# Layer ends rebuilt in a Hawk / latent-attention / PEER trunk on one core: quarter tiles, squares on GpSimd, later weight splits, rotation inside the scores' contraction

## The chip, the core and the metric

The kernel runs on one core of a Trainium2 chip. A core has TensorE (PE, with its weight loads shown apart as PEld), VectorE (DVE), ScalarE (ACT), GpSimd (POOL), SyncE (SP, which here only starts transfers) and 16 DMA engines. The metric is the time of one execution on the device in microseconds; it was run three times before the change, and once more under the profiler.

## The reference

512 tokens of 1024 channels pass through one recurrent layer (RG-LRU), a PEER layer, one latent-attention layer (MLA) and a second PEER layer. Each sub-layer normalises its input, scales and shifts it by a conditioning vector ("ada"), and adds its result, times a gate, to the stream x. Cut to what the change touches:

```python
for l in range(2):
    mod = silu(c) @ ada_w[l] + ada_b[l]           # 6 x 1024: sh1 sc1 g1 sh2 sc2 g2
    h = rmsnorm(x, norm_mix_g[l]) * (1 + sc1) + sh1
    y = rglru_block(h) if l == 0 else mla_block(h)
    x = x + g1 * y
    h = rmsnorm(x, norm_ffn_g[l]) * (1 + sc2) + sh2
    x = x + g2 * peer(h)
return rmsnorm(x, final_g)

# mla_block, 16 heads of 64 + 32 query channels over a shared latent
q = (rmsnorm(h @ w_dq) @ w_uq)                    # q_nope 64, q_rope 32
s = (q_nope @ k_nope.T + rope(q_rope) @ rope(k_rope).T) * SCALE
# peer, 8 heads: 16 best of 128 x 128 experts by product keys
out = sum_k  g_k * gelu(h . u[idx_k]) * v[idx_k]
```

## The kernel before, in words

All values are kept transposed: channels on the 128 partitions, 512 tokens along the row, so x is eight tiles of 128x512. Matrix products are done in float32 by three passes (`mm3`, lines L187 to L189): each operand is split into a high part, rounded by ACT (L162, `whi`, `vh`, `hh`), and a low part, the difference, made by DVE or POOL (L163, `wlo`, `vl`, `hl`); PE multiplies high by low, low by high, high by high into one bank. `wtile` loads a weight tile and splits it; `split` is the split alone.

The work is written as five stages in a row, rglru, peer0, mla, peer1 and final. A scheduler with a model of each engine's times sets each engine's order from the dependences, the buffer counts and a few anchors (`tc.issue_after(instruction)` keeps what stands in it behind that instruction, on the same engine).

A norm needs the sum of squares over all 1024 channels. `residual` (L282) adds a bank's result into one tile of x, `sum_sq` squares the tile on ACT (L224, L225: `nacc`, `sq`) and adds it to `nacc` on DVE (L226); when all eight are in, `col_sums` sums over the partitions on PE (L232, `st`), ACT takes the square root (L243, `rcol`), DVE the reciprocal (L244), and PE spreads it to all partitions (L247, `rs`). Then DVE normalises (L257, `xn`), and ACT and DVE make `hh` and `hl`, the operands of the next product. This chain stands at the end of each stage, and the next stage's matmuls need it.

At the end of **rglru** (about 100 to 206 us of the span) PE makes per head the two gates' inputs (`ri`) and, between heads, an output gate (`gate`), then the output product (`wo`). DVE meanwhile runs the recurrence, and after the last split of y ten rows of the ada product: each loads 512 KB (`ada_raw`) and reduces 128x1024 against c (`ada_junk`, L151), with two buffers. Two weight tiles of the next stage (`wpq0`, 128x1024) are split by ACT and DVE there.

**peer** scores the keys (`pq`), takes the best 16, builds gates, computes expert activations in a dense form (`u`) and sums values: 128 value tiles `vraw` are loaded by SP, split, and multiplied by the split activations `al`, `ah` into six banks `acc` (three blocks of 128 tokens by two halves of 512 channels; the fourth block, `gacc`, is gathered by POOL and summed on DVE). Of the last two tiles ("held") the first half is multiplied at once and the second half after it; then `emit` copies the banks to `onat` (ACT and DVE), `finish(c)` transposes one of eight column blocks on PE (`ot`), adds it into x and squares it. Other work is spread over peer0's value loop: ada rows, and `positions` (`ps_...`), which makes the rotation's table and the mask and writes them to scratch in memory.

**mla** multiplies the normalised x to latents, rotates the shared 32 key channels, then for each of 16 heads makes q (`q`), rotates it, splits it to `qt`, and multiplies with `kt` (the scores, `s`, a contraction of 96 rows: 64 plain, 32 rotated). The 32 rotated channels come twice out of the product, plain in rows 64 to 95 and with halves swapped in rows 96 to 127; the rotation is rows 64 to 95 times a cosine table, plus rows 96 to 127 times a sine table: ACT copies `q` to `qf` (L644), then three operations of 32x512 follow (L646 to L648), on DVE for the first two heads and on POOL for the others. POOL also makes the low parts of mla's weights.

Of the kernel before, what the change touches and what calls it, by code (L numbers as in the profile page):

```python
# [9 lines left out]
F32 = mybir.dt.float32  # L10
# [39 lines left out]
HT = 8  # L50
RAWS = 4
GROWS = 4
LAST = 2
WF = 2
GSCALE = 16384.0

# [25 lines left out]
class Trunk:  # L82
# [137 lines left out]
    def sum_sq(self, sq, ch, k):  # L220
# [4 lines left out]
        last = nc.scalar.activation(sq, ch, AF.Square).ins  # L225
        nc.vector.tensor_tensor(self.nacc, self.nacc, sq, op=OP.add)  # L226
        return last

    def col_sums(self):
        self.sums = self.bank("st")  # L230
# [104 lines left out]
    def rglru(self):  # L335
        nc, io, tc = self.nc, self.io, self.tc
        with tc.tile_pool(name="lru", bufs=52) as pool, ExitStack() as st:
# [87 lines left out]
            ys = []  # L425
            for hd in range(4):
                gates(hd)
                gate(3 + hd)
                for j in (2 * hd, 2 * hd + 1):
                    last = decay(j)  # L430
                if hd == 3:
                    gate(KC - 1)
                if hd % 2 == 0:
                    continue
                js = range(2 * hd - 2, 2 * hd + 2)
                for j in js:
                    with tc.issue_after(last):
                        last2 = nc.scalar.activation(tt[j], tt[j], AF.Sqrt, scale=-1.0, bias=self.tiny).ins
                for j in js:
                    nc.vector.tensor_tensor(tt[j], tt[j], rr[j], op=OP.mult)  # L440
                    nc.vector.tensor_tensor(tt[j], tt[j], ig[j], op=OP.mult)
                    nc.vector.tensor_tensor_scan(tt[j], aa[j], tt[j], initial=0.0, op0=OP.mult, op1=OP.add)
                    with tc.issue_after(last2):
                        last_gelu = nc.scalar.activation(gg[j], gg[j], AF.Gelu).ins
                    nc.vector.tensor_tensor(tt[j], tt[j], gg[j], op=OP.mult)
                    ys.append(self.pair(pool, "y"))
                    lo = self.split(ys[j][0], ys[j][1], tt[j]).ins
            with tc.issue_after(conv):
                self.adas(6, late)
            with tc.issue_after(lo):  # L450
                self.adas(10, late)
            outs = [self.bank("wo") for _ in range(KC)]
            ws = []
            for k in range(KC):
# [90 lines left out]
    def mla(self):  # L545
        nc, io, tc = self.nc, self.io, self.tc
        with tc.tile_pool(name="mla", bufs=12) as pool, ExitStack() as st:
# [4 lines left out]
            mb = one([P, NB, T], BF, "mask_b")  # L552
            ckv = [(one([P, T], F32R, f"ckvh{m}"), one([P, T], F32R, f"ckvl{m}")) for m in range(2)]
            qlat = [(one([P, T], F32R, f"qlh{m}"), one([P, T], F32R, f"qll{m}")) for m in range(3)]
            nc.scalar.dma_start(rt, self.rscr)
            nc.scalar.dma_start(mb, self.mscr)
            gk = self.gain("gs_kv", self.vecr("kv_norm_g", 0, KC), self.mod[:, 104:112])
            gs = self.gain("gs_m1", self.vecr("norm_mix_g", KC, KC), self.mod[:, 56:64])
# [1 line left out]
            with tc.tile_pool(name="mlah", bufs=34) as hp:  # L560
                xn, hk = [], []
                for k in range(KC):
                    xn.append(self.normed(hp, k, rs))
                    hk.append(self.affine(hp, k, xn[k], gk, self.mod[:, 96:104])[1])
                    if k == KC - 2:
                        after = self.last
                outs = [self.bank("lat"), self.bank("lat"), self.bank("kr")]
                self.lin_k(outs[:2], [self.wtile(io["w_dkv"][m], KC, eng=nc.vector) for m in range(2)], hk)
                self.lin(outs[2], self.wtile(io["w_kr"], KC, eng=nc.vector), hk)
                wdq = [self.wtile(io["w_dq"][m], KC, pool=hp) for m in range(2)]  # L570
                krf = pool.tile([P, T], F32, name="krf", tag="t")
                nc.scalar.activation(krf, outs[2], AF.Copy)
                with tc.issue_after(after):
                    hq = [self.affine(hp, k, xn[k], gs, self.mod[:, 48:56], None if k < 6 else self.pair(pool, "hm"), 0, True)[1]
                          for k in range(KC)]
                kr2 = pool.tile([P, T], F32, name="kr2", tag="t")
                nc.gpsimd.tensor_tensor(kr2[64:96], krf[96:128], rt[96:128], op=OP.mult)
                nc.gpsimd.tensor_tensor(krf[64:96], krf[64:96], rt[64:96], op=OP.mult)
                nc.gpsimd.tensor_tensor(krf[64:96], krf[64:96], kr2[64:96], op=OP.add)
                lats = [self.bank("lat") for _ in range(3)]  # L580
                self.lin(lats[0], wdq[0], hq)
                with tc.issue_after(self.latent_sums(pool, outs[:2])):
                    self.lin(lats[1], wdq[1], hq)
                self.latent_norm("kv_latent_g", ckv)
                self.lin(lats[2], self.wtile(io["w_dq"][2], KC), hq)
# [36 lines left out]
            values_load(1)  # L622
            values(0)
            self.latent_sums(top, lats)
            kts = [pool.tile([96, 2, T], F32R, name=f"kt{i}", bufs=1) for i in range(4)]
            keys(0)
            self.latent_norm("q_latent_g", qlat)
            self.preload(AF.Exp, self.last_sqrt)

            def rope_rows(n):  # L630
                for kt in kts[n:n + 2]:
                    self.split(kt[64:96, 0, :], kt[64:96, 1, :], krf[64:96], nc.gpsimd)

            rope_rows(0)
            att, ots, qts, pns, pts, norms = [], {}, {}, {}, {}, {}
# [1 line left out]
            def proj(hd):  # L637
                if hd % 2 == 0 and hd > 2:
                    keys(hd // 2)
                qps = self.bank("q")  # L640
                self.last_q = self.lin(qps, self.wtile(io["w_uq"][hd], 3), qlat)
                qf = pool.tile([P, T], F32, name="qf", bufs=1)
                t2 = pool.tile([96, T], F32, name="qr2", bufs=1)
                nc.scalar.activation(qf, qps, AF.Copy)  # L644
                eng = nc.gpsimd if hd > 1 else nc.vector
                eng.tensor_tensor(t2[64:96], qf[96:128], rt[96:128], op=OP.mult)  # L646
                eng.tensor_tensor(qf[64:96], qf[64:96], rt[64:96], op=OP.mult)
                eng.tensor_tensor(qf[64:96], qf[64:96], t2[64:96], op=OP.add)  # L648
                qt = pool.tile([96, 2, T], F32R, name="qt", bufs=3)
                self.split(qt[:, 0, :], qt[:, 1, :], qf[:96], eng)  # L650
                qts[hd] = qt

            def scores(hd):
# [3 lines left out]
                for b in range(NB):  # L657
# [4 lines left out]
                    nc.vector.tensor_tensor_reduce(p, sp, mb[:, b, :], op0=OP.add, op1=OP.max, scale=SCALE,  # L662
                                                   scalar=FMIN, accum_out=st[:, 0, b:b + 1])
                    pns[hd].append(p)
                nc.vector.tensor_scalar(st[:, 1, :], st[:, 0, :], -1.0, None, op0=OP.mult)
                for b, p in enumerate(pns[hd]):
                    self.last_exp = nc.scalar.activation(p, p, AF.Exp, bias=st[:, 1, b:b + 1], accum_out=st[:, 2, b:b + 1]).ins
                nc.vector.reciprocal(st[:, 3, :], st[:, 2, :])
# [196 lines left out]
    def peer(self, l):  # L865
        nc, io, tc = self.nc, self.io, self.tc
        nd = NB - 1
        with ExitStack() as st:
# [4 lines left out]
            vs = [gat.tile([P, 16, TOPK], F32, name=f"v{b}") for b in range(NB)]  # L873
            iu = [gat.tile([P, 16, TOPK], U32, name=f"iu{b}") for b in range(NB)]
            gs = self.gain(f"gs_f{l}", self.vecr("norm_ffn_g", KC * l, KC), self.mod[:, mo + 32:mo + 40])
            rs = self.rstd(D)
# [149 lines left out]
            def v_load(t):  # L1026
                raw = self.wp.tile([P, D], F32, name="vraw", tag="raw", bufs=RAWS)
                nc.sync.dma_start(raw, io["v"][l * P + t])
                if t < P - LAST:
# [4 lines left out]
                vls.append(self.split(vh, vl, raw).ins)  # L1034
                return vh, vl

            def v_part(t, f, a, v):
                fs = slice(f * T, f * T + T)
                for b in range(nd):
                    bs = slice(b * P, b * P + P)  # L1040
                    last = self.mm3(acc[b][f], (a[0][:, bs], a[1][:, bs]), (v[0][:, fs], v[1][:, fs]), t == 0, t == P - 1)
                return last.ins

            acc, held = None, []
# [33 lines left out]
            self.preload(AF.Sqrt)  # L1078

            sqs = vp.tile([P, NSG, WG * TG], F32, name="sqs", tag="wt").rearrange("p a b -> p (a b)").rearrange("p (c t) -> p c t", t=T)  # L1080

            def emit(f):
                for b in range(nd):
                    o = outs[b][:, f * T:f * T + T]
                    if b == 1:
                        nc.vector.tensor_copy(o, acc[b][f])
                    else:
                        nc.scalar.activation(o, acc[b][f], AF.Copy)
# [158 lines left out]
```

## Time and profile before

| what | value |
|---|---|
| median of three runs | 3117.28 us (3113.58 to 3120.99) |
| the profiled execution | 3117.19 us, span 3115.4 us, mean granted clock 0.98 |
| PE busy | 2987.1 us, 96% of the span |
| DVE, ACT, POOL busy | 82%, 44%, 29% |
| transfers | 821 MB, mean 264 GB/s |
| rglru's end: `st` begins | 205.95 us |
| mla's end: `st` waits | 5.8 us |
| peer0's and peer1's end: `st` waits | 4.1 us each |

How to read it: PE is nearly always busy, so time is found only where PE stands still or runs at a lower clock. A row such as "PE st L232 <- DVE nacc L226: 45.5, 7, 15.2" says that PE's instruction `st` of line 232 stood idle 45.5 us in all, 7 times, at most 15.2, until DVE's `nacc` of line 226 was done. In a row of the timeline stand start, duration, engine, line, operation, output and inputs, count, and in brackets the idle time before it and what ended it.

### The profile page before, as it was taken

The numbers are of one execution on the slowest core, as the hardware profiler recorded it, in microseconds if no ns is written. First come the engines' busy times: TensorE is split into PE (matmuls) and PEld (weight loads), VectorE is DVE, ScalarE is ACT, GpSimd is POOL, SyncE is SP. The second block draws the span as 40 slices with busy tenths as digits, with TensorE's granted clock in tenths as the row PEclk, the third lists the DMA queues.
The fourth block names the chain that finished last, engine by engine and source line by source line (L and its number), as shares of the span: only waits on it lengthen the run. The fifth ranks groups of instructions, "written<-read, shape, count | busy, mean of one in ns | idle before, by whom it ended". The sixth has DMA issues, their size and how long they took to land. (4 is left out here: it accounts for less than half of the span.)

```text
span 3115.4 us, 43400 instructions
## 1 busy us (share of the span) xinstructions
PE 2987.1 (96%) x15462; PEld 2648.1 (85%) x15462; DVE 2565.5 (82%) x4848; ACT 1385.4 (44%) x1974; POOL 900.8 (29%) x700
## 2 busy tenths in 40 slices
PE   7979999999999999999899989999999999999997
PEld 5669999999887889998677779999999788889996
DVE  8879999898797778888668768999886787778886
ACT  5643255655343333333566642355655333333333
POOL 4000004342223215545256500014432221134440
PEclk9989999999999999999899989999999999999998
DMA  8454568998999999999213244469998999999994
GB/s 298 130 171 146 176 213 304 317 340 315 357 329 357 347 313 354 343 344 331 66 50 112 72 150 135 134 221 332 317 336 310 374 344 315 321 320 340 337 334 139
DMA packets 345112, 821.15 MB, mean 264 GB/s; under 512 B 33600, under 2 KB 179136, under 8 KB 338496
## 3 DMA queue, kind: packets, MB, share of 16 engines
q1 hardware_dynamic: 239632, 460.91, 44.3%
q0 software_dynamic: 73728, 268.47, 24.3%
q10 hardware_dynamic: 31536, 89.00, 7.5%
q8 instruction: 122, 2.00, 0.3%
q14 instruction: 94, 0.77, 0.1%
HBM read 730.98 MB, written 87.29 MB: 263 GB/s over the span
## 5 line engine op out<-in xcount | busy, mean ns | idle before, releaser
L1132 POOL DMA_INDIRECT grow<-in_u_dram,idx x256 | 343.4, 1341 | 1287.0 <-DVE oh L804 651.7
L187 PE MATMUL u<-hh,wlo 128*128 128x384 f32 x2048 | 690.9, 337 | 3.0 <-ACT gsp L914 3.0
L189 PE MATMUL u<-hh,whi 128*128 128x384 f32 x2048 | 688.0, 336 | 0.0
L188 PE MATMUL u<-hl,whi 128*128 128x384 f32 x2048 | 686.9, 335 | 0.0
L188 PE MATMUL acc<-vl,ah 128*128 128x512 f32 x1536 | 601.1, 391 | 0.1
L189 PE MATMUL acc<-vh,ah 128*128 128x512 f32 x1536 | 600.8, 391 | 0.0
L1132 POOL DMA_INDIRECT grow<-in_v_dram,idx x256 | 366.4, 1431 | 681.1 <-DVE gacc L1141 389.4
L187 PE MATMUL acc<-vh,al 128*128 128x512 f32 x1536 | 544.9, 392 | 14.6 <-ACT vh L162 10.5
L163 DVE TENSOR_TENSOR wlo<-raw,whi 128x1024 fp32r<-128x1024 f32 x315 | 383.7, 1219 | 103.2 <-ACT whi L162 101.1
L163 DVE TENSOR_TENSOR vl<-vraw,vh 128x1024 fp32r<-128x1024 f32 x256 | 313.3, 1224 | 146.9 <-ACT vh L162 142.6
L162 ACT ACTIVATE whi<-raw 128x1024 fp32r<-128x1024 f32 (+2 forms) x372 | 358.4, 965 | 145.1 <-PE u L189 29.0
L187 PEld LDWEIGHTS u<-hh,wlo 128*128 128x128 f32 x2048 | 386.2, 189 | 6.5 <-ACT gsp L914 3.7
L188 PEld LDWEIGHTS u<-hl,whi 128*128 128x128 f32 x2048 | 386.1, 189 | 2.7
L189 PEld LDWEIGHTS u<-hh,whi 128*128 128x128 f32 x2048 | 385.6, 188 | 0.0
L187 PEld LDWEIGHTS acc<-vh,al 128*128 128x128 f32 x1536 | 290.3, 189 | 75.8 <-ACT vh L162 12.2
L188 PEld LDWEIGHTS acc<-vl,ah 128*128 128x128 f32 x1536 | 289.9, 189 | 60.2 <-DVE vl L163 0.9
L189 PEld LDWEIGHTS acc<-vh,ah 128*128 128x128 f32 x1536 | 289.4, 188 | 60.6
L1141 DVE SCALAR_TENSOR_TENSOR gacc<-grow,gdot,gacc 128x1024 f32<-128x1024 f32 x254 | 325.0, 1279 | 14.6 <-DMA grow<-in_v_dram,idx 13.3
L162 ACT ACTIVATE vh<-vraw 128x1024 fp32r<-128x1024 f32 x256 | 268.6, 1051 | 137.0 <-issue 51.8
L1136 DVE CUSTOM_DVE_ANT_0 grow<-grow,hn 128x1024 f32<-128x1024 f32 x256 | 308.6, 1220 | 13.1 <-DMA grow<-in_u_dram,idx 12.8
L162 ACT ACTIVATE ah<-gact 128x384 fp32r<-128x384 f32 x180 | 94.2, 523 | 332.2 <-PE acc L189 186.7
L860 ACT ACTIVATE stg<-wps 128x512 f32<-128x512 f32 x192 | 186.9, 1106 | 54.5 <-PE wps L857 40.8
(349 smaller groups left out, 4257.5 us busy)
## 6 DMA issues: line engine op xcount, KB each, us to landing
raw<-in_uT_dram SPq DMA_DIRECT2D x256, 512.0 KB
vraw<-in_v_dram SPq DMA_DIRECT2D x256, 512.0 KB
ada_raw<-in_adaw_dram SPq DMA_DIRECT2D x112, 512.0 KB
wscr<-stg ACTq DMA_DIRECT2D x48, 1024.0 KB
wt<-wscr SPq DMA_DIRECT2D x32, 1536.0 KB
gscr<-gsp ACTq DMA_DIRECT2D x152, 192.0 KB
gact<-gscr SPq DMA_DIRECT2D x110, 192.0 KB
raw<-in_w_pq_dram SPq DMA_DIRECT2D x32, 512.0 KB
```

Of the source, the lines that this page charges most:

```text
L162: nc.scalar.activation(hi, src, AF.Copy)
L163: return (eng or nc.vector).tensor_tensor(lo, src, hi.bitcast(F32), op=OP.subtract)
L187: nc.tensor.matmul(out, al, bh, start=first, stop=False)
L188: nc.tensor.matmul(out, ah, bl, start=False, stop=False)
L189: return nc.tensor.matmul(out, ah, bh, start=False, stop=last)
L860: nc.scalar.activation(stg[:, :, c:c + 4].rearrange("p e t -> p t e"), wps.rearrange("p (t e) -> p t e", t=4), AF.Copy, scale=1.0 / GSCALE)
L1132: nc.gpsimd.indirect_dma_start(out=row, out_offset=None, in_=tabs[s], in_offset=bass.IndirectOffsetOnAxis(ap=idx[:, k:k + 1], axis=0))
L1136: nc.vector.tensor_tensor_reduce(row, row, hn, op0=OP.mult, op1=OP.add, scale=1.0, scalar=0.0, accum_out=col)
L1141: nc.vector.scalar_tensor_tensor(acc, row, col, acc, op0=OP.mult, op1=OP.add)
```

## The change

It has five parts. (1) In rglru the output gates 3 and 4 are computed after heads 0 and 2 and the gates 5 to 7 after head 3; the last ada rows get a third buffer. (2) At both places where peer begins, three instead of two first weight tiles with three banks; their low parts are made behind the last add of squares. (3) At the end of peer three value tiles are held; their second half is multiplied by quarters of 256 columns with transposes between, the last quarter into banks `rest` of its own, added by DVE; of the seven adds of squares four are done by POOL; the square root's table is asked for right behind the first copies. (4) In mla the rotation's table gets ones in its first 64 rows and one DVE multiplication makes all 128 rows of `qf` straight from the bank; the sum of cosine and sine part is left to the contraction, which has 128 rows with the rotated keys standing in it twice. The small negation of the row maxima goes from DVE to ACT. (5) Nothing else is written differently, but the scheduler sets other orders elsewhere too.

```diff
-LAST = 2
+LAST = 3
@@ rglru
-                gate(3 + hd)
+                if hd % 2 == 0:
+                    gate(3 + hd // 2)
...
                 if hd == 3:
-                    gate(KC - 1)
+                    for m in range(5, KC):
+                        gate(m)
...
             with tc.issue_after(lo):
-                self.adas(10, late)
+                self.adas(10, late, bufs=3)
@@ mla
-            nc.scalar.dma_start(rt, self.rscr)
+            nc.vector.memset(rt[:64], 1.0)
+            nc.scalar.dma_start(rt[64:], self.rscr[64:])
...
+                nc.gpsimd.tensor_copy(krf[96:128], krf[64:96])
...
-                nc.scalar.activation(qf, qps, AF.Copy)
-                eng = nc.gpsimd if hd > 1 else nc.vector
-                eng.tensor_tensor(t2[64:96], qf[96:128], rt[96:128], op=OP.mult)
-                eng.tensor_tensor(qf[64:96], qf[64:96], rt[64:96], op=OP.mult)
-                eng.tensor_tensor(qf[64:96], qf[64:96], t2[64:96], op=OP.add)
-                qt = pool.tile([96, 2, T], F32R, name="qt", bufs=3)
-                self.split(qt[:, 0, :], qt[:, 1, :], qf[:96], eng)
+                nc.vector.tensor_tensor(qf, qps, rt, op=OP.mult)
+                qt = pool.tile([P, 2, T], F32R, name="qt", bufs=3)
+                self.split(qt[:, 0, :], qt[:, 1, :], qf, nc.gpsimd if hd > 1 else nc.vector)
...
-                nc.vector.tensor_scalar(st[:, 1, :], st[:, 0, :], -1.0, None, op0=OP.mult)
+                nc.scalar.activation(st[:, 1, :], st[:, 0, :], AF.Copy, scale=-1.0)
@@ peer, its beginning
-            pq0 = [self.bank("pq"), self.bank("pq")]
-            wpq0 = [self.wtile(io["w_pq"][l * 16 + m], KC, eng=nc.vector) for m in range(2)]
+            pq0 = [self.bank("pq") for _ in range(3)]
+            wpq0 = []
+            for m in range(3):
+                with tc.issue_after(last_nacc), tc.issue_after(last_sq) if m else ExitStack():
+                    wpq0.append(self.wtile(io["w_pq"][l * 16 + m], KC, eng=nc.vector))
@@ peer, its end
-                self.sum_sq(sqs[:, c % 6, :], self.x[:, c, :], c)
+                self.sum_sq(sqs[:, c % 6, :], self.x[:, c, :], c, nc.gpsimd if c < KC - 3 else nc.vector)
...
-            emit(0)
+            self.preload(AF.Sqrt, emit(0))
+            for i, (t, pair) in enumerate(held):
+                with tc.issue_after(last):
+                    last = v_part(t, 1, *pair, 0, 2 * P)
+                if i:
+                    with tc.issue_after(last):
+                        last = finish(i - 1)
+            emit(1)
+            rest = [self.bank("rest")[:, :2 * P] for _ in range(nd)]
+            for i, (t, pair) in enumerate(held):
+                with tc.issue_after(last):
+                    last = v_part(t, 1, *pair, 2 * P, 2 * P, rest)
+                if i < 2:
+                    with tc.issue_after(last):
+                        last = finish(2 + i)
+            for b in range(nd):
+                o = outs[b][:, 6 * P:]
+                nc.vector.tensor_tensor(o, o, rest[b], op=OP.add)
             with tc.issue_after(last):
-                for t, pair in held[:-1]:
-                    v_part(t, 1, *pair)
-            done = [finish(c) for c in range(KC // 2)][1]
-            with tc.issue_after(done):
-                v_part(P - 1, 1, *held[-1][1])
-            emit(1)
-            for c in range(KC // 2, KC):
-                finish(c)
+                for c in range(4, KC):
+                    finish(c)
```

How the instructions move. First DVE at the end of rglru, before (`gs_f` is the next norm's gain, `wlo` the splits of the next stage's first weights):

```order
L282 SCALAR_TENSOR_TENSOR x<-wo,mod,x 128x512
L163 TENSOR_TENSOR wlo<-raw,whi 128x1024
L226 TENSOR_TENSOR nacc<-nacc,sq 128x512
L163 TENSOR_TENSOR wlo<-raw,whi 128x1024
L278 SCALAR_TENSOR_TENSOR gs_f_1562<-mod,vecs 128x8
L226 TENSOR_TENSOR nacc<-nacc,sq 128x512 x4
L244 RECIPROCAL rcol<-rcol 128x4
```

and after:

```order
L226 TENSOR_TENSOR nacc<-nacc,sq 128x512
L282 SCALAR_TENSOR_TENSOR x<-wo,mod,x 128x512
L226 TENSOR_TENSOR nacc<-nacc,sq 128x512 x3
L163 TENSOR_TENSOR wlo<-raw,whi 128x1024 x3
L244 RECIPROCAL rcol<-rcol 128x4
```

The splits stand behind the adds now, three of them, ahead of the reciprocal. Next DVE at the end of peer1, before (`onat` are the copies of the banks, `ot` the transposes):

```order
L1086 COPY onat_28669<-acc_23146 128x512
L282 SCALAR_TENSOR_TENSOR x<-ot,mod,x 128x512 x2
L1086 COPY onat_28669<-acc_23147 128x512
L226 TENSOR_TENSOR nacc<-nacc,sqs 128x512
L282 SCALAR_TENSOR_TENSOR x<-ot,mod,x 128x512 x3
L226 TENSOR_TENSOR nacc<-nacc,sqs 128x512
L282 SCALAR_TENSOR_TENSOR x<-ot,mod,x 128x512
L226 TENSOR_TENSOR nacc<-nacc,sqs 128x512
```

and after:

```order
L1088 COPY onat_28622<-acc_23118 128x512
L282 SCALAR_TENSOR_TENSOR x<-ot,mod,x 128x512 x3
L1120 TENSOR_TENSOR onat_28621<-onat_28621,rest 128x256
L1120 TENSOR_TENSOR onat_28622<-onat_28622,rest 128x256
L1120 TENSOR_TENSOR onat_28623<-onat_28623,rest 128x256
L282 SCALAR_TENSOR_TENSOR x<-ot,mod,x 128x512 x4
L226 TENSOR_TENSOR nacc<-nacc,sqs 128x512 x3
```

Four columns' additions to x stand ahead of the three new adds, four behind; four adds of squares have left DVE (they stand on POOL), and the last three are together at the end. Last POOL in the middle of mla, before (`qr` and `qf` are the rotation of one head, `osl` the low part of a head's output):

```order
L646 TENSOR_TENSOR qr_15530<-qf,rope_t 32x512
L647 TENSOR_TENSOR qf<-qf,rope_t 32x512
L163 TENSOR_TENSOR wlo<-raw,whi 128x384
L163 TENSOR_TENSOR osl<-ot,osh 128x512
L648 TENSOR_TENSOR qf<-qf,qr_15530 32x512
L163 TENSOR_TENSOR qt<-qf,qt 96x512
```

and after:

```order
L163 TENSOR_TENSOR wlo<-raw,whi 128x256 x2
L163 TENSOR_TENSOR wlo<-raw,whi 128x384
L163 TENSOR_TENSOR qt<-qf,qt 128x512
L163 TENSOR_TENSOR osl<-ot,osh 128x512
L163 TENSOR_TENSOR wlo<-raw,whi 128x256 x3
```

The three small operations are gone; POOL has the splits alone. In peer0's value loop, SP's loads of the value tiles and of the position work stand in another order than before.

More of the change, by code (lines that the diff above doesn't have):

```diff
@@ L218, in preload, with sum_sq @@
             self.nc.scalar.activation(warm, self.eps, func)
-    def sum_sq(self, sq, ch, k):
+    def sum_sq(self, sq, ch, k, eng=None):
         nc = self.nc
@@ L224, in sum_sq @@
             return nc.scalar.activation(self.nacc, ch, AF.Square).ins
-        last = nc.scalar.activation(sq, ch, AF.Square).ins
-        nc.vector.tensor_tensor(self.nacc, self.nacc, sq, op=OP.add)
-        return last
+        self.last_sq = nc.scalar.activation(sq, ch, AF.Square).ins
+        self.last_nacc = (eng or nc.vector).tensor_tensor(self.nacc, self.nacc, sq, op=OP.add).ins
+        return self.last_sq
     def col_sums(self):
@@ L448, in rglru @@
             with tc.issue_after(conv):
-                self.adas(6, late)
+                self.adas(6, late, bufs=3)
             with tc.issue_after(lo):
-                self.adas(10, late)
+                self.adas(10, late, bufs=3)
             outs = [self.bank("wo") for _ in range(KC)]
@@ L624, in mla @@
             self.latent_sums(top, lats)
-            kts = [pool.tile([96, 2, T], F32R, name=f"kt{i}", bufs=1) for i in range(4)]
+            kts = [pool.tile([P, 2, T], F32R, name=f"kt{i}", bufs=1) for i in range(4)]
             keys(0)
@@ L631, in rope_rows @@
                 for kt in kts[n:n + 2]:
-                    self.split(kt[64:96, 0, :], kt[64:96, 1, :], krf[64:96], nc.gpsimd)
+                    self.split(kt[64:, 0, :], kt[64:, 1, :], krf[64:], nc.gpsimd)
             rope_rows(0)
@@ L641, in proj @@
                 self.last_q = self.lin(qps, self.wtile(io["w_uq"][hd], 3), qlat)
-                qf = pool.tile([P, T], F32, name="qf", bufs=1)
-                t2 = pool.tile([96, T], F32, name="qr2", bufs=1)
-                nc.scalar.activation(qf, qps, AF.Copy)
-                eng = nc.gpsimd if hd > 1 else nc.vector
-                eng.tensor_tensor(t2[64:96], qf[96:128], rt[96:128], op=OP.mult)
-                eng.tensor_tensor(qf[64:96], qf[64:96], rt[64:96], op=OP.mult)
-                eng.tensor_tensor(qf[64:96], qf[64:96], t2[64:96], op=OP.add)
-                qt = pool.tile([96, 2, T], F32R, name="qt", bufs=3)
-                self.split(qt[:, 0, :], qt[:, 1, :], qf[:96], eng)
+                qf = pool.tile([P, T], F32, name="qf", bufs=2)
+                nc.vector.tensor_tensor(qf, qps, rt, op=OP.mult)
+                qt = pool.tile([P, 2, T], F32R, name="qt", bufs=3)
+                self.split(qt[:, 0, :], qt[:, 1, :], qf, nc.gpsimd if hd > 1 else nc.vector)
                 qts[hd] = qt
@@ L875, in peer @@
             gs = self.gain(f"gs_f{l}", self.vecr("norm_ffn_g", KC * l, KC), self.mod[:, mo + 32:mo + 40])
+            last_nacc, last_sq = self.last_nacc, self.last_sq
             rs = self.rstd(D)
             h = []
-            pq0 = [self.bank("pq"), self.bank("pq")]
-            wpq0 = [self.wtile(io["w_pq"][l * 16 + m], KC, eng=nc.vector) for m in range(2)]
+            pq0 = [self.bank("pq") for _ in range(3)]
[3 more added lines that the diff above has]
+                    wpq0.append(self.wtile(io["w_pq"][l * 16 + m], KC, eng=nc.vector))
             with tc.tile_pool(name=f"tmp{l}", bufs=8) as tmp:
@@ L1028, in v_load @@
                 nc.sync.dma_start(raw, io["v"][l * P + t])
-                if t < P - LAST:
+                if t < P - 2:
                     vh = self.wp.tile([P, D], F32R, name="vh", tag="whi")
@@ L1035, in v_load, with v_part @@
                 return vh, vl
-            def v_part(t, f, a, v):
-                fs = slice(f * T, f * T + T)
+            def v_part(t, f, a, v, c=0, n=T, to=None):
+                fs = slice(f * T + c, f * T + c + n)
                 for b in range(nd):
                     bs = slice(b * P, b * P + P)
-                    last = self.mm3(acc[b][f], (a[0][:, bs], a[1][:, bs]), (v[0][:, fs], v[1][:, fs]), t == 0, t == P - 1)
+                    out, t0 = (to[b], P - LAST) if to else (acc[b][f][:, c:c + n], 0)
+                    last = self.mm3(out, (a[0][:, bs], a[1][:, bs]), (v[0][:, fs], v[1][:, fs]), t == t0, t == P - 1)
                 return last.ins
@@ L1077, in peer @@
             g2 = self.mod[:, mo + 40:mo + 48]
-            self.preload(AF.Sqrt)
             sqs = vp.tile([P, NSG, WG * TG], F32, name="sqs", tag="wt").rearrange("p a b -> p (a b)").rearrange("p (c t) -> p c t", t=T)
@@ L1087, in emit @@
                     else:
-                        nc.scalar.activation(o, acc[b][f], AF.Copy)
+                        last = nc.scalar.activation(o, acc[b][f], AF.Copy)
+                return last.ins
             def finish(c):
```

## The prediction

> **What bounds the kernel now.** I read the page's busy shares first, then the view of PE's waits, then windows over the stretches in which PE stands still.
>
> ```profile
> span 3115.4 us, 43400 instructions
> PE 2987.1 (96%) x15462; PEld 2648.1 (85%) x15462; DVE 2565.5 (82%) x4848; ACT 1385.4 (44%) x1974; POOL 900.8 (29%) x700
> PE st L232 <- DVE nacc L226: 45.5, 7, 15.2
> PE acc L187 <- ACT vh L162: 10.5, 4, 4.5
> PE wo L187 <- POOL wlo L163: 5.0, 1, 5.0
> PE q L187 <- POOL wlo L163: 2.4, 2, 1.6
> PE tp L677 <- ACT qf L644: 1.4, 2, 0.7
> PE s L187 <- DVE qt L163: 0.7, 1, 0.7
> ```
>
> PE is busy for 2987 of 3115 us. The change removes next to no matmul, so all it can win lies in the 128 us in which PE is not busy, and in work that runs at a lowered clock. The columns of the waits are total, times and longest. The largest entry is the start of the column sums ("st") waiting for the last add of squares ("nacc"): 45.5 us over seven norms. That is the place the change is aimed at, at four of the seven: the end of rglru, both peer ends, the end of mla. The wait of 15.2 is the kernel's start, which the change leaves alone. The next rows are the windows at rglru's end, in peer0's value loop and in the last third of mla (busy time by engine, granted clock, DMA share, GB/s):
>
> ```profile
> 192.00:206.00 14.00, 0.05 (x1) 0.08 (x1) 13.29 (x20) 5.45 (x8) 0.00 (x0) 0.56 0.60 209
> 850.00:1000.00 150.00, 140.54 (x592) 114.96 (x593) 128.17 (x201) 56.09 (x73) 39.47 (x26) 0.95 0.99 349
> 1700.00:1815.00 115.00, 101.11 (x491) 77.41 (x489) 81.57 (x153) 66.58 (x149) 55.18 (x52) 0.94 0.30 96
> ```
>
> At rglru's end PE does nothing for 14 us while DVE is busy 13.29 of them: DVE is the bound there.
>
> **Part 1, the end of rglru** (weight splits behind the last add, a third buffer for the ada rows, gates in another order). DVE there (the wait is of 170 to 195):
>
> ```profile
> DVE ada_junk L151 <- DMA ada_raw<-in_adaw_dram: 7.0, 5, 2.5
> 170.00:180.00 10.00, 10.00 (x46) 8.29 (x45) 5.85 (x9) 1.24 (x3) 0.00 (x0) 1.00 0.77 240
> 199.78 1.22 DVE L163 TENSOR_TENSOR wlo<-raw,whi 128x1024 fp32r<-128x1024 f32 x1
> 201.51 1.22 DVE L163 TENSOR_TENSOR wlo<-raw,whi 128x1024 fp32r<-128x1024 f32 x1
> 202.73 3.07 DVE L226 TENSOR_TENSOR nacc<-nacc,sq 128x512 f32<-128x512 f32 x4
> 208.12 0.18 DVE L244 RECIPROCAL rcol<-rcol 128x4 f32<-128x4 f32 x1 [2.32 <-ACT rcol L243]
> ```
>
> Two splits of 1.22 stand ahead of the last adds; moved behind, they give 2.44. Three splits now lie between the last add and the reciprocal: 3 x 1.22 = 3.66, where DVE had 2.32 to spare, so the reciprocal comes 1.3 late. Net 1.1. The third ada buffer aims at DVE's waits for the ada transfers, five of them, 7.0 us. The transfer engines are 0.77 busy there, so I let about a fifth of the 24 us from 170 to 194 be squeezed out: 4.8. Against it: the gates. Sixteen matmuls for two heads now stand together ahead of a gate, and gates 5 to 7 behind the last head's; by the order PE then stands for a gate bank that ACT has yet to empty. I estimate 3.2 us on PE: a table load (1.28) and three ops of 0.63 on ACT, by rows that stand in part 3. PE's own end may move (14 us are free there), but the ada loads are held until the last split of y, and I let 1.9 of the 3.2 reach that, since DVE and ACT work on meanwhile. That comes to 1.1 + 4.8 - 1.9 = **4**. Ends: none of the transfer wait won, 1.1 - 1.9 = -0.8; all won and y not late, 8.1. The third "pq" bank and third weight I cost at nothing: PE has a matmul for every bank from there on, and if the bank were missed PE would wait one eviction, under 1 us. The extra load of a third weight joins SP's queue in the same place as before; the load is not added, only its split is.
>
> **Part 2, the end of mla.** The same edit.
>
> ```profile
> 1811.10 2.35 DVE L163 TENSOR_TENSOR wlo<-raw,whi 128x1024 fp32r<-128x1024 f32 x2
> 1813.37 1.48 DVE L226 TENSOR_TENSOR nacc<-nacc,sq 128x512 f32<-128x512 f32 x2
> PE st L232 <- DVE nacc L226: 5.8, 1, 5.8
> ```
>
> Two splits (2.35) go behind the adds, and by the order a third that stands further ahead (1.22, as at rglru's end): 3.5 earlier, less 1.4 for the reciprocal that then has three splits ahead of it: **2.1**, between 1 (only the two count) and 3.5 (the splits find room beside the sums).
>
> **Part 3, both ends of peer** (they are alike; this is peer1's, the chain in order of time):
>
> ```profile
> 3092.02 0.40 PE L189 MATMUL acc<-vh,ah 128*128 128x512 f32 x1
> 3093.24 1.40 DVE L282 SCALAR_TENSOR_TENSOR x<-ot,mod,x 128x512 f32<-128x512 f32 x2
> 3096.72 0.68 DVE L226 TENSOR_TENSOR nacc<-nacc,sqs 128x512 f32<-128x512 f32 x1
> 3096.84 0.63 ACT L225 ACTIVATE sqs<-x 128x512 f32<-128x512 f32 x1 [0.63 <-DVE x L282]
> 3101.66 1.83 PE L232 MATMUL st<-ones,nacc 128*128 128x1 f32 x8 [4.14 <-DVE nacc L226]
> 3103.58 1.28 ACT L243 ACT_TABLE_LOAD   x1 [3.53 <-PE st L232]
> 3104.87 0.26 ACT L243 ACTIVATE rcol<-st,eps 128x4 f32<-128x4 f32 x1
> 1573.37 0.39 PE L189 MATMUL q<-qlh,whi 128*128 128x512 f32 x1
> 1573.60 0.28 PE L187 MATMUL v<-wuvh,ckvl 128*128 128x256 f32 x1
> 1576.35 0.28 PE L189 MATMUL v<-wuvh,ckvh 128*128 128x256 f32 x1
> L163 POOL TENSOR_TENSOR osl<-ot,osh x8: 1272/1280/1289, 1612.1 to 1798.0; 128x512 fp32r<-128x512 f32 x8
> L163 POOL TENSOR_TENSOR qt<-qf,qt x14: 1281/1391/2281, 1592.6 to 1767.6; 96x512 fp32r<-96x512 f32 x14
> ```
>
> Let L = 3092.25 be when the last accumulating matmul leaves PE's queue. Today DVE needs from L to 3101.66, or 9.4, because x (0.70 each) and nacc (0.68) of six columns take turns on it. After the change the first four columns are through before L, and PE pays for it: 54 matmuls of 256 columns for 27 of 512 (the 24 of "v" from 1573.60 to 1576.35 start 0.12 apart, the 512-wide one ahead of them 0.23: 6.5 us for 6.2, at most 0.4 more) and eight more transposes ahead of L, 1.0 at the price of a 256-wide one. Behind L stand three adds of "rest" (128x256, estimated at 0.42 each from the 0.68 of 512, 1.3), four x at 0.70, 0.7 for the last square on ACT and its hand-over, 0.8 for the last add and the start of st, and some 0.8 for the first hand-over from PE: 1.3 + 2.8 + 0.7 + 0.8 + 0.8 = 6.4. So st at L + 1.4 + 6.4 = L + 7.8, which is 1.6 earlier. Without the hand-over, which the adds of "rest" may cover, it would be 2.4: I take the middle, 2.0. The four adds on POOL cost 1.28 each by the row of "osl", the nearest POOL op of that shape; they run beside DVE's x, and the fourth ends about 3.9 after L (1.3 + 0.7 for the first x, 0.63 for its square, 1.28), just ahead of DVE's first add at 4.1 (1.3 + 2.8). Then the table: the function's table is loaded at 3103.58, on the path, since nothing before it on ACT asks for the square root; now a one-element square root stands right behind the first copies out of PSUM, and the load of 1.28 lies beside matmuls. 2.0 + 1.28 = 3.3 an end, **6.6** for both. Ends: 1 each (POOL adds at the 2281 of the slowest "qt" with ACT's squares late too) and 4.5 each.
>
> [...]
>
> **Part 4, mla's rotation** (one DVE multiply from PSUM replaces ACT's copy and three small ops, mostly on POOL):
>
> ```profile
> L646 POOL TENSOR_TENSOR qr<-qf,rope_t x14: 1260/1266/1286, 1587.9 to 1759.2; 32x512 f32<-32x512 f32 x14
> L648 POOL TENSOR_TENSOR qf<-qf,qr x14: 1267/1287/1297, 1590.6 to 1764.0; 32x512 f32<-32x512 f32 x14
> L188 PE MATMUL s<-kt,qt x64: 387/389/398, 1576.7 to 1780.8; 96*128 96x512 f32 x64
> 1760.53 1.26 POOL L647 TENSOR_TENSOR qf<-qf,rope_t 32x512 f32<-32x512 f32 x1
> 1761.86 2.10 POOL L163 TENSOR_TENSOR wlo<-raw,whi 128x256 fp32r<-128x256 f32 x3
> ```
>
> POOL loses 14 x 3 x 1.27 = 53 us, DVE gains 16 x 0.68 = 11 and loses six ops of 0.68, ACT loses 16 copies and gains 16 tiny negates. The contraction of 128 rows instead of 96 costs PE nothing that I can see: a score over 96 rows takes 389 ns, and a value matmul over 128 rows (3092.02) took 0.40. None of POOL's 53 us is on the path but where PE waits for POOL: the 5.0 for "wlo" (two rotation ops of 1.26 stood ahead of it, so 2.5), half of 2.4 for the queries' "wlo" (1.2), the 0.7 for the scores' operand: 4.4, less 0.4 for a DVE that is 71% busy there. **4**. Ends: 0, if ACT's high parts are last anyway; 11.5, if all four waits (9.5) and about 2 us of slow clock behind the long one go (the window's 0.94 over 115 us is 6.9 us of clock, and most of it fell on a standing PE). One small POOL copy and one memset come ahead of the first scores, and DVE's first two heads lose three ops each; what hides the copy is the latent norm behind which those scores stand, and without that cover it costs 1.3.
>
> **Part 5, a side effect.** The scheduler puts peer0's position work and loads into another order. Three of the four waits of "acc" for "vh" (10.3 of 10.5, the first row, of 840 to 1000) lie where transfers are the bound (share 0.99) and SP's queue, in order, stood behind two late operands:
>
> ```profile
> PE acc L187 <- ACT vh L162: 10.3, 3, 4.5
> SPq L1054 <- DVE gdot L1136: 11.0, 3, 10.4
> SPq L473 <- DVE gacc L1141: 9.2, 1, 9.2
> ```
>
> The same loads are issued in a new order. I can't tell the sign: **0**, between 10 lost and 14 won.
>
> **Sum.** 4 + 2.1 + 6.6 + 4 + 0 = 16.7. The profiled execution took 3117.19 (span 3115.4 and 1.8 around it), and the median of the runs is 3117.28. 3117.2 - 16.7 = **3100.5**.
>
> **The rivals.**
> - *Peer0's stalls go.* The 10.3 us and what the clock lost behind them. The window's clock of 0.95 over 150 us is 7.5 us of full clock, about half of it while PE worked: 14 in all, so 3086. For it: the position work that blocked SP stands elsewhere. Against: the transfer share stays 0.99, and the same bytes have to come.
> - *Hardly any change.* The ada transfers come no faster (-0.8), mla's end gives 1, the peer ends 1 each and the rotation nothing, as ACT is last: 2.2, so 3115. For it: DMA 0.77 busy, and POOL ops that stretch to 2281.
> - *Slower.* One mechanism: in peer0's value loop the new order of SP's queue makes a load wait behind a DVE result more often. Each such stall costs as the three did: 10.3 / 3 + 3.6 / 3 = 4.6. Five of them eat the sum (23 against 16.7 + 6.2); with six the time is 3100.5 + 27.6 = 3128. For it: the queue's two long waits. Against: the bytes are the same, and vraw loads stand ahead of the position loads in one place and behind in another.
>
> **How the numbers follow.** My forecast, a gain of 7 to 28: 0.64. The first rival (more than 28): 0.11. Hardly any change (0 to 7): 0.19. The slower one: 0.06. Less than 0.2% (6.2 us) is what a measurement here can't tell from none; three quarters of the third case (0.14) and the small losses of the last (0.01) lie within: 0.15. Slower by more: 0.05. Faster by more: 0.64 + 0.11 + 0.05 = 0.80. For the range I leave out gains over 31 and under 3: 3086 to 3114. The likeliest case alone has 3089 to 3110.
>
> **What would show it.** At rglru's end the ada rows should no longer wait for their transfer, st should start near 200 instead of 205.95, and the reciprocal should follow it with the three splits between. At the peer ends the table load should stand before the last value matmuls and st should wait 2 us or less. The waits "wo <- wlo" should halve. Round 850 to 1000 "acc <- vh" shows which of the three rivals holds: none, about 10, or 20 and more. I am wrong if the last POOL add ends after DVE's adds, if gates 5 to 7 make y later than 2 us, or if DVE becomes last in mla.

## The result and the profile after

The changed kernel took 3100.44 us (median of four runs, 3099.3 to 3100.85) against 3117.0 before: the ratio is 0.9946, 95% interval 0.9929 to 0.9963. A later run on another chip gave 0.9947 (0.9934 to 0.9961). The forecast was 3100.5. The total was right, but two of its terms were not, as the last part shows.

The page of the kernel after, span and busy shares:

```profile
span 3098.8 us, 43500 instructions
PE 2980.4 (96%) x15516; PEld 2642.5 (85%) x15516; DVE 2557.2 (83%) x4841; ACT 1381.6 (45%) x1974; POOL 860.2 (28%) x667
```

Rows of its view of PE's waits (total, times, longest):

```profile
PE st L232 <- DVE nacc L226: 33.3, 7, 15.3
PE acc L187 <- ACT vh L162: 9.1, 4, 6.6
PE rs L247 <- DVE rcol L244: 6.1, 5, 2.4
PE ri L406 <- ACT gate L396: 5.2, 1, 5.2
PE acc L187 <- DVE al L163: 4.5, 5, 1.7
PE pq L187 <- DVE wlo L163: 2.8, 2, 1.4
PE gate L187 <- ACT g L408: 1.7, 1, 1.7
PE q L187 <- POOL wlo L163: 1.6, 1, 1.6
PE wo L187 <- POOL wlo L163: 0.4, 1, 0.4
```

"st" lost 12.2 us of its waits (45.5 to 33.3) and "wo <- wlo" 4.6. The largest rows that are new or longer: "ri" for "gate" 5.2, "gate" for "g" 1.7, "pq" for "wlo" 2.8, and "acc" for "al" 4.5. Two things that the list and the cut diff of the change do not show belong to it: the rotated head `qf` has two buffers instead of one, and the six ada rows ahead of the last ones get the third buffer too.

To see what each part gave, take the start of the same PE instruction in both timelines and the stretches between such starts ("rs" is the spread of a norm's root to all partitions). In us, before, after, and the difference:

| stretch | before | after | difference |
|---|---|---|---|
| start to rglru's "rs" | 208.35 | 208.93 | +0.6 |
| to peer0's first "u" | 29.74 | 31.51 | +1.8 |
| to its first "acc" | 568.88 | 566.55 | -2.3 |
| to the "rs" behind peer0 | 702.50 | 703.62 | +1.1 |
| to mla's last "wo" | 299.33 | 285.89 | -13.4 |
| to the "rs" behind mla | 8.60 | 6.56 | -2.0 |
| to peer1's first "acc" | 602.30 | 603.31 | +1.0 |
| to the last "rs" | 685.71 | 682.43 | -3.3 |
| to the end | 10.01 | 10.00 | 0.0 |

They sum to -16.6 before rounding, and 13.4 of that is in mla. Single traces scatter: the second trace of the changed kernel differs from this one by up to 1.9 us in a stretch (mla took 283.99 there), and in kernels that leave rglru as it was its "rs" stands anywhere from 206.2 to 208.4.

### The profile page after: what moved, and what is told of

Same layout as the page of the kernel before. It is cut to its first block, busy times and chain, and to the rows that moved or that the text cites. A ratio compares the mean times of both kernels' runs of the same rounds, so it can differ in the third digit from the quotient of the medians.

```text
span 3098.8 us, 43500 instructions
## 1 busy us (share of the span) xinstructions
PE 2980.4 (96%) x15516; PEld 2642.5 (85%) x15516; DVE 2557.2 (83%) x4841; ACT 1381.6 (45%) x1974; POOL 860.2 (28%) x667
## 4 chain that ended last, share of the span: by engine, by line
PE 82%; DVE 7%; DMA 6%; issue 3%; ACT 2%; POOL 1%; DVEq 0%; ACTq 0%; SPq 0%; POOLq 0%
PE u L187 11%; PE u L188 11%; PE u L189 11%; PE acc L188 10%; PE acc L187 10%; PE acc L189 10%; PE wps L856 6%; PE pq L187 2%; PE pq L188 2%; PE pq L189 2%; DMA vraw<-in_v_dram 2%; DMA ada_raw<-in_adaw_dram 2%; DVE ada_junk L151 1%; PE sc L963 1%; DVE wlo L163 1%
## 5 line engine op out<-in xcount | busy, mean ns | idle before, releaser
L188 PE MATMUL acc<-vl,ah 128*128 128x512 f32 x1536 | 598.6, 390 | 1.4 <-DVE vl L163 1.4
L1155 DVE SCALAR_TENSOR_TENSOR gacc<-grow,gdot,gacc 128x1024 f32<-128x1024 f32 x254 | 324.8, 1279 | 12.2 <-DMA grow<-in_v_dram,idx 10.0
```

The lines of the kernel that those rows point to most:

```text
L188: nc.tensor.matmul(out, ah, bl, start=False, stop=False)
L1155: nc.vector.scalar_tensor_tensor(acc, row, col, acc, op0=OP.mult, op1=OP.add)
```

## The experiments: the parts alone

Each kernel is the one before with one part of the change. The edits are the lines of the diff above; the rotation's also has the second buffer of `qf`.

**The rotation** (the lines under mla: ones in the table, rows 96 to 127 of the keys, one multiply, negation on ACT).

> The kernel before with part 4 alone (rotation in the contraction, negation on ACT). Theory: mla's gain between the two norms' spreads, 15 us in the traces of before and after, is the rotation's own but for 2 of the later splits: 3117 - 13 = 3104 (3101 to 3107), with the 5.0 of wo for wlo gone and the time from the last q to the last wo near 44 instead of 53.6. Rival: the rotation gives the 4 of the prediction and the rest of mla's gain comes from other parts by another order: 3113.

It took 3103.33; ratio 0.995 (0.9933 to 0.9966), 15.6 us. The theory holds: the part alone does it, and in its trace the stretch to mla's last "wo" is 14.3 shorter than before, with 43.9 from the last "q" to the last "wo" instead of 53.6. PE's waits in mla before (window 1566 to 1812):

```profile
PE wo L187 <- POOL wlo L163: 5.0, 1, 5.0
PE q L187 <- POOL wlo L163: 2.4, 2, 1.6
PE pv L187 <- ACT pth L162: 2.3, 1, 2.3
PE wo L187 <- ACT osh L162: 2.3, 2, 2.1
PE tp L677 <- ACT qf L644: 1.4, 2, 0.7
PE q L188 <- DVE qll L163: 1.3, 1, 1.3
PE s L187 <- DVE qt L163: 0.7, 1, 0.7
PE tp L677 <- ACT p L667: 0.5, 3, 0.2
```

and with the rotation alone (those of the norm behind mla, which fall into the window here, left out):

```profile
PE wo L187 <- ACT osh L162: 2.1, 1, 2.1
PE q L187 <- POOL wlo L163: 1.6, 1, 1.6
PE q L188 <- DVE qll L163: 1.3, 1, 1.3
PE s L187 <- ACT ot L693: 1.1, 1, 1.1
PE wo L188 <- POOL osl L163: 1.0, 2, 0.6
PE wo L187 <- POOL wlo L163: 0.4, 1, 0.4
PE pv L187 <- ACT pth L162: 0.3, 1, 0.3
```

**The peer ends** (LAST = 3, quarters, rest, four adds on POOL, the early table).

> The kernel before with part 3 alone (quarters, rest banks, four adds on POOL, the table asked for early). Theory: 3.3 us at each peer end, and nothing in peer0's value loop: 3110.4. Rival: peer0's value loop is put in another order by this part and loses 3 to 4 us in its waits for vh and al, as in the trace after: 3114.

3113.35; 0.9986 (0.9976 to 0.9996), 4.4 us by the ratio. In its trace the stretch from the first "acc" to the "rs" is 3.5 shorter at peer0 and 3.4 at peer1. So the ends give what the forecast had (3.3 each); together they are 6.9, which the interval of the ratio (1.2 to 7.5 us) includes. That part alone did not lengthen peer0's stretch; the rival falls.

**The later weight splits** (three weights, anchors).

> The kernel before with part 2 alone (three first weights, their splits behind the last add). Theory: mla's end gains 2; at rglru's end the reciprocal waits for three splits, and pq waits 1.4 us for the third low part at both places: 2 + 1.1 - 2.8, so within 1 us of 3117. Rival (the prediction's terms): 1.1 + 2.1 without a price for the third weight, 3113.8.

3114.36; 0.9996 (0.9986 to 1.0006). The ratio says no difference, as the theory had it, but its interval (4.4 us faster to 1.9 slower) holds the rival's 3.2 as well, so the time does not decide. The trace speaks for the theory: mla's last "wo" to its "rs" -2.4, then +1.0 until "u" (the third weight's low part), and "rs" comes 1.0 later behind "st" at both places.

**The gates' order and the third ada buffer.**

> The kernel before with the gates' order and the third ada buffer alone. Theory: PE stands 6.9 us for ACT in the gates, wo ends 6.5 later, and the adas start 5 to 6 later, so the buffer's gain of up to 5 is eaten: 3117 to 3119. Rival (the prediction): 4.8 of transfer waits won against 1.9: 3114.

3126.19; 1.0026 (1.0015 to 1.0037): 8 us slower, more than either theory. Its PE (window 100 to 240):

```profile
PE st L232 <- DVE nacc L226: 9.1, 1, 9.1
PE ri L406 <- ACT gate L396: 3.6, 1, 3.6
PE gate L187 <- ACT g L408: 2.6, 1, 2.6
```

PE stands 6.2 us in the gates, the last "wo" begins 7.0 later and "rs" 1.8 later; 5.2 more came up to the first "acc", in peer0, where nothing of this part stands. The four parts sum to 15.6 + 4.4 + 1.2 - 8.1 = 13.1; the whole gave 16.6. With intervals of 3 to 5 us to either side on each, that difference needs no cause.

## The experiments: what was to be undone

**The old gate order in the changed kernel**, `gate(3 + hd)` behind each head and the last gate behind head 3, and then two ada buffers as well.

```diff
-                if hd % 2 == 0:
-                    gate(3 + hd // 2)
+                gate(3 + hd)
...
-                    for m in range(5, KC):
-                        gate(m)
+                    gate(KC - 1)
```

> The changed kernel with the gates in the old order (gate 3 + head behind each head), all else changed, the third ada buffer too. Theory: the new order is a loss in itself, as the kernel before with gates and buffer alone was 8 us slower: without it PE's 6.9 us of waits for ACT go, wo ends near 191 and the sums of rglru's end start near 200; 3100.4 - 6 = 3094 (3090 to 3096). Rival: the 8 us were mostly peer0's order, which each build sets anew, and only the 1.3 us seen at rglru's end are the gates': 3099.

> The changed kernel with the gates in the old order and two ada buffers. Theory: the third buffer takes away most of the 7.0 us in which DVE waits for the ada transfers at rglru's end, so this is 3 to 5 us above the one with three buffers: 3097 to 3099. Rival: the transfers are bound by their rate and not by the buffers, and both come out alike: within 1 us.

With three buffers: 3097.09 on a chip where the kernel before took 3119.22, 0.9927 (0.9911 to 0.9944), which of 3117 is 3094, as the first theory had it. The interval overlaps that of the changed kernel and just holds the rival's 3099, so the trace has to decide. With two: 3097.85, 0.9929 (0.9912 to 0.9946). DVE's waits around rglru's end (7.0 before, by the row in the prediction), first in the changed kernel:

```profile
DVE ada_junk L151 <- DMA ada_raw<-in_adaw_dram: 4.4, 5, 1.3
```

in the old order with three buffers:

```profile
DVE ada_junk L151 <- DMA ada_raw<-in_adaw_dram: 4.5, 4, 1.4
```

and with two:

```profile
DVE ada_junk L151 <- DMA ada_raw<-in_adaw_dram: 7.9, 5, 2.9
```

"rs" at rglru's end stands at 202.7 with three buffers, 206.3 with two, 208.9 in the changed kernel. So at that place the old order gives 6.2 and the third buffer 3.6, both as expected; but the times with two and three buffers are alike, as the rival had it for another reason. The stretch from "rs" to peer0's first "acc" took 602.3 with three and 598.7 with two: what the buffer won ahead of peer0 was gone at its first "acc" (805.0 in both).

**All adds of squares on DVE** in the changed kernel (`self.sum_sq(..., c)`, without GpSimd).

> The changed kernel with all adds of squares on DVE. Theory: DVE stands idle 0.75 us behind each of the first columns' x, so three of the four adds of 0.68 fit there, and only one lands behind the last x: 0.7 an end, 1.4 in all: 3102. Rival (as the prediction counted): the four adds lie in the chain, 2.7 an end: 3106.

3107.36; 0.9956 (0.9939 to 0.9973), with runs from 3099.8 to 3110.5, so the times alone decide nothing. The trace does: "st" starts 1.7 and 1.6 later behind the last value matmul than in the changed kernel, between the two theories' 0.7 and 2.7. POOL's adds in the changed kernel, and the end of the chain on DVE:

```profile
3077.91 1.30 POOL L226 TENSOR_TENSOR nacc<-nacc,sqs 128x512 f32<-128x512 f32 x1 [30.59 <-PE ot L1096]
3082.65 1.28 POOL L226 TENSOR_TENSOR nacc<-nacc,sqs 128x512 f32<-128x512 f32 x1 [0.38 <-ACT sqs L225]
3080.10 1.07 DVE L1120 TENSOR_TENSOR onat<-onat,rest 128x256 f32<-128x256 f32 x3
3081.09 2.91 DVE L282 SCALAR_TENSOR_TENSOR x<-ot,mod,x 128x512 f32<-128x512 f32 x4
3083.96 2.28 DVE L226 TENSOR_TENSOR nacc<-nacc,sqs 128x512 f32<-128x512 f32 x3
```

The fourth POOL add ends at 3083.93, DVE's first starts at 3083.96: just in time, as forecast, and none of these four is stretched. The table load stands at 3072.93, ahead of the last value matmul (3080.19), also as forecast:

```profile
3072.93 1.28 ACT L218 ACT_TABLE_LOAD   x1
3088.26 0.26 ACT L243 ACTIVATE rcol<-st,eps 128x4 f32<-128x4 f32 x1 [3.54 <-PE st L232]
```

## The experiments: why the rotation gave 14 us and not 4

**POOL made busy again**: the rotation in the contraction, with work that feeds nothing put back.

```diff
+                if hd > 1:
+                    t2 = pool.tile([96, T], F32, name="idle", bufs=1)
+                    for _ in range(3):
+                        nc.gpsimd.tensor_tensor(t2[64:96], qf[64:96], rt[64:96], op=OP.mult)
```

> The kernel before with the rotation in the contraction, and three idle multiplications of 32x512 put back on POOL for each of the last 14 heads, on a tile that nothing reads. Their work is extra and feeds nothing. Theory: mla gained because POOL came free for the weights' low parts, so with POOL as busy as before the wait of wo for wlo comes back and half or more of the 14 us is lost: 3110 or more. Rival: it gained because the chain from q to qt is four operations shorter, and POOL's load is beside the point: 3103 to 3105.

3103.68; 0.9948 (0.9932 to 0.9965). With POOL as loaded as before (135.4 us busy from 1566 to 1812, against 132.7), all the gain is still there. Its profiled execution was its slowest, 3110.56, and even there mla's stretch was 10.7 shorter than before. The amount of POOL's work is not the cause.

**The old rotation on DVE for all heads** (`eng = nc.vector`, the split left where it was).

> The kernel before with the rotation's three operations on DVE for all heads instead of POOL for 14 of them; operations and their order in the chain stay four. Theory: the length of the chain from q to qt is what the heads wait for; with DVE at 0.68 instead of POOL at 1.27 it is 1.8 us shorter of the 3.8 that the contraction saves, so about half of the 15 us: 3110. Rival: the count of operations on the busy DVE matters, and 28 us more on DVE in mla, which is over 70% busy, eat the gain: 3117 or more.

3116.82; 1.0002 (0.9993 to 1.0011). No gain, as the rival had it.

**The same idle work on DVE** (`nc.vector` in the lines above).

> The kernel before with the rotation in the contraction, and three idle multiplications of 32x512 on DVE for each of the last 14 heads, on a tile that nothing reads, so that DVE does in mla about what it did with the whole rotation on it, and q's chain stays short. Theory: the rotation on DVE brought nothing because its 28 us of work on the busy DVE cost what the shorter chain won: this is 3110 or more. Rival: the heads wait for the number of operations in a row between q and qt, not for any engine's load: 3103 to 3106, as with the idle work on POOL.

3113.25; 0.9979 (0.997 to 0.9988): 6.5 of 15.6 us are left. The window 1566 to 1812 of the kernel before:

```profile
1566.00:1812.00 246.00, 228.64 (x1154) 178.26 (x1154) 181.31 (x355) 152.44 (x340) 132.68 (x119) 0.97 0.27 85
```

of the old rotation on DVE:

```profile
1566.00:1812.00 246.00, 229.98 (x1154) 176.53 (x1154) 205.18 (x395) 151.94 (x337) 83.23 (x76) 0.98 0.26 82
```

and of the idle work on DVE:

```profile
1566.00:1812.00 246.00, 229.55 (x1160) 177.60 (x1158) 214.69 (x392) 149.51 (x341) 83.31 (x77) 0.98 0.28 85
```

The columns are PE, PEld, DVE, ACT, POOL (busy us and instructions), clock, DMA share, GB/s. So 29 us of idle work on DVE cost 9 us, and the same operations on POOL, where they take 54 us, none. In mla's heads added work counts on DVE and not on POOL. That fits with the rotation on DVE bringing nothing: it has 24 us more on DVE (205 against 181).

What is left is that the change takes three operations out of q's path and adds little to DVE (16 multiplies for six old operations and 16 negations). Before, the path went from ACT to POOL and back to ACT, and each stood waiting for the other. POOL's row (window 1490 to 1815), and the copy and the rotation that stood ahead of the low part for which PE waited the 5.0 us:

```profile
POOL qr L646 <- ACT qf L644: 30.3, 11, 4.4
1758.56 0.57 ACT L644 ACTIVATE qf<-q 128x512 f32<-128x512 f32 x1
1759.21 1.26 POOL L646 TENSOR_TENSOR qr<-qf,rope_t 32x512 f32<-32x512 f32 x1 [3.55 <-ACT qf L644]
```

POOL stood 30.3 us for ACT's copies, and ACT 14.7 us for POOL's rotated rows; in the changed kernel ACT waits 2.0 us for DVE's product and POOL 1.8 for q's high part. This shows where the waiting was, not what removed it: the rotation's part also frees 16 copies on ACT, moves the negations to ACT and gives `qf` a second buffer, and none of these was run alone. How much of the 14 us is the shorter path stays open.

## A version that beats both

The old gate order, three ada buffers, and of the three later splits the third behind the reciprocal:

```diff
-                with tc.issue_after(last_nacc), tc.issue_after(last_sq) if m else ExitStack():
+                with tc.issue_after(self.recip if m == 2 else last_nacc), tc.issue_after(last_sq) if m else ExitStack():
```

> The changed kernel with the gates in the old order and the third weight's split behind the reciprocal (two splits fit into DVE's 2.32 us ahead of it, the third into its 1.21 us behind it). Theory: the old order gains 6 us at rglru's end and the moved split 1.0 at each of two ends, together 8 against the changed kernel, of which peer0 may take back up to 4: 0.992 of before, 3092 to 3096. Rival: peer0's loads set the time to its value loop, so that whatever is gained ahead of it is lost again: equal to the changed kernel but for 1 us at mla's end.

> The changed kernel once more, beside the two below and the kernel before on one chip: 0.9946 of before, as it was, and in the trace the stretch from rglru's spread of the root to peer0's first value matmul again 598 us if the build sets it, or up to 4 us off if it changes from one execution to the next.

3089.74 against 3100.63 for the changed kernel on the same chip; of before 0.9908 (0.9893 to 0.9923) and 0.9947 (0.9934 to 0.9961). The intervals do not touch. The gain over the changed kernel, 10.9 us, is more than the 8 expected and rules out the rival's 1. Its DVE at rglru's end shows the two splits that fit ahead of the reciprocal and the one behind it:

```profile
195.83 3.06 DVE L226 TENSOR_TENSOR nacc<-nacc,sq 128x512 f32<-128x512 f32 x4
198.81 2.35 DVE L163 TENSOR_TENSOR wlo<-raw,whi 128x1024 fp32r<-128x1024 f32 x2
201.22 0.18 DVE L244 RECIPROCAL rcol<-rcol 128x4 f32<-128x4 f32 x1
201.31 1.20 DVE L163 TENSOR_TENSOR wlo<-raw,whi 128x1024 fp32r<-128x1024 f32 x1
202.60 0.69 DVE L257 TENSOR_TENSOR xn<-x,rs 128x512 f32<-128x512 f32 x1
```

"rs" is at 201.5 instead of 208.6 in the changed kernel's second trace, yet peer0's first "acc" is no earlier (808.0 against 807.5): by there all of it was gone, as the rival had it. Against that second trace the rest of the profiled execution was 1.1 shorter at mla's end, as aimed at, and, where nothing was aimed at, 3.6 shorter in peer0 behind the first "acc", 5.1 longer in mla and 5.3 shorter from mla's "rs" to peer1's first "acc". It was also the slowest of its four runs (3096.04), so where the timed runs gained is not seen. The changed kernel's own stretch from "rs" to "acc" came out alike in both its traces (598.1 and 598.9), as if the build set it.

## Why the prediction was right, and where it was not

The total came out within 0.1 us, and that is luck: part 4 gave 9.4 us more than forecast, and part 1 (6.4 less), the third weight behind part 2 (1.1) and peer0's value loop (2.1) took it away again. By the steps:

- **Part 1, forecast 4, measured a loss of 2.4 up to peer0's "u"** (+0.6 and +1.8 in the table). With rglru as it was "u" begins at 236.0 to 238.1 in six traces, and in three with the changed order at 240.4 to 240.7, so it is a loss of 2.3 to 4.7. The step that failed is the price of the gates: "I estimate 3.2 us on PE ... and I let 1.9 of the 3.2 reach that". PE stood 5.2 + 1.7 = 6.9 us, the ada rows began 5.6 later (175.72 for 170.11), and only 2.6 of the transfers' 7.0 us were won, not 4.8. The prediction's own sign of being wrong, y later than 2 us, came true; "st" began at 205.5 and not near 200. The second step is "The third 'pq' bank and third weight I cost at nothing": "pq" waited 1.4 for its low part, at both places. The splits' delay of the reciprocal was right: 1.0 for 1.3. Experiments: gates and buffer alone 8 us slower, the old order 6.2 earlier at that place.
- **Part 2, forecast 2.1, measured 2.0** at mla's end, with 1.0 lost behind it up to peer1's first "acc", where "pq" waited 1.4 for the third weight.
- **Part 3, forecast 3.3 an end, measured 3.3** at peer1, and 3.5 and 3.4 with the part alone. Inside: the table 1.3 as counted (from the start of "st" to the root 3.21 before and 1.87 after, at peer1); POOL's adds 1.6 by taking them away. "st" still waited 3.2, though the sign was 2 or less; it began 6.1 behind the last value matmul, where the sum had 6.4. Seven of the eight adds took 1.27 to 1.30 on POOL against 0.68 on DVE, and still they pay: POOL had been idle 30.6 us ahead of them at peer1 and 18.9 at peer0. The eighth, the second at peer0, took 1.94, while DVE had a weight split that took 1.48 and not 1.22; the fourth there still ended at 1505.72, just ahead of DVE's first add at 1505.75.
- **Part 4, forecast 4, measured 13.4**, beyond its upper end of 11.5. The mis-sized term is PE's waits: I let half of "wo <- wlo", half of "q <- wlo" and "s <- qt" go, 4.4. In fact mla's waits fell from 15.9 (the list of before, under the rotation's experiment) to 7.3, by 8.6, with some I had not touched ("pv <- pth" 2.3 to 0.3). The waits were priced one by one as POOL's work ahead of a low part, and POOL made busy again shows that its work was not what counted. Most of the rest is the clock behind two waits, of which the sum had nothing and only the upper end 2:

```profile
1755.00:1770.00 15.00, 10.05 (x43) 7.92 (x42) 7.50 (x15) 7.79 (x19) 8.55 (x9) 0.77 0.17 54
1797.00:1812.00 15.00, 11.22 (x39) 8.06 (x39) 11.26 (x16) 9.24 (x17) 5.79 (x6) 0.87 0.51 165
```

  Those are of before, around the waits of 5.0 and 2.1. Read in steps of 1 us, the clock stood at half (0.50) from 1760.4 to 1767.2, and PE worked in the last 4.6 us of that; and from 1798.0 to 1801.4, with PE at work throughout. Matmuls began 0.43 us apart there instead of 0.23, so about half of 4.6 and of 3.4 us was lost, an estimated 4.0 in all. (What the clock lost while PE stood still is part of the wait and costs nothing more.) After, the first of the two windows is at full clock:

```profile
1755.00:1770.00 15.00, 15.00 (x85) 12.12 (x84) 11.06 (x25) 9.45 (x22) 4.50 (x5) 1.00 0.12 35
```

  8.6 + 4.0 = 12.6 of the 13.4; the last 0.8 has no row. When the clock falls the traces do not settle: the second fall came behind a wait of 2.1 us, and after the same wait of 2.1 us in the changed kernel (1784.1 to 1786.2) the clock stayed at 1.00. And "a DVE that is 71% busy" was priced at 0.4: the idle work on DVE shows it at 9 us for 29.
- **Part 5, forecast 0 between -10 and 14, measured** 2.3 won up to the first "acc" and about 4.4 lost in the value loop (1.1 more up to "rs", although the end itself gave 3.3). The row "acc <- vh" fell from 10.5 to 9.1, and "acc <- al" and "acc <- vl" added 5.3. Neither the first rival nor the third came; the sign stayed open for good reason: builds that change nothing in peer0 differ by up to 5 us from "rs" to the first "acc" (598.6 before, 603.8 with the gates alone).
- "Hardly any change" was wrong in every item but rglru's end.

## What to carry to other kernels

Price a wait of PE by its length and by the time that PE then works at the lowered clock: here, by the estimate above, the wait of 5.0 us was worth about 7.3, and a wait of 2.1 about 3.8 in one kernel and 2.1 in the other. On a stage whose engines hand each other small operations, look at who waits for whom along that path before counting how much work each engine has: idle work was free on POOL, which it took from 31% to 55% busy, and cost a third of its time on DVE, which it took from 75% to 87%. And test the parts of a change apart: here one part of five was 8 us slower by itself and hidden by the rest.

## What the runs showed that was not expected

Time won ahead of peer0 need not reach its value loop. From "rs" behind rglru to peer0's first "acc" the changed kernel and its versions took 598 to 607 us, and those that began earliest took longest ("rs" at 201.5 and 202.7: 606.5 and 602.3 us; at 206.3 to 208.9: 598 to 599). Among the kernels made from the one before there is no such order (598.8 to 603.8, with "rs" at 205.3 to 210.2). Which resource sets that point was not tried; the transfer share from 500 to 800 is 0.93 to 0.94 in the kernel before, the changed one and its versions.
